# One hybrid mLSTM encoder layer: the seventh block product gets a PSUM bank of its own, and log sigmoid's series runs on 128 partitions behind the first plain pair

## The chip, the cores and the metric

One Trainium2 chip, of which the kernel uses one core. The metric is the device time of one execution in microseconds (us); lower is better. A run of the program gives one time, and the profiler's execution gives a time of its own beside the trace.

## The reference, cut to what matters

A layer of a streaming encoder works on 512 prompt and 32 sample rows (544 in all) of 2048 features, in float32. `h` is the normed and modulated input, and one combined projection `proj = h @ w_in` gives q, k, v, o, z_a, the input and forget gates (2 x 4 columns), u, z_b, g_a and g_b. Two things of it matter here.

```python
ig = ifg[..., :N_HEADS_A].transpose(0, 2, 1)
lf = jax.nn.log_sigmoid(ifg[..., N_HEADS_A:]).transpose(0, 2, 1)   # one value per head and row: 4 x 544
...
b = jnp.cumsum(lf, axis=-1)          # per chunk; b, ig and a running max m set all weights of the mLSTM
proj = jnp.einsum('bld,de->ble', h, w_in)                          # 2048 x 14344 weights
```

Everything behind that (mLSTM, pooling mixer, two branches, output projection, norm) is left as it is by the change.

## The kernel before, in words

The 2048 features lie on 16 tiles of 128 partitions, the 544 rows along the free dimension in two halves of 272. Each float32 operand is split into a rounded high part and a low part (`split`, L91: ScalarE casts the high part, L92, VectorE subtracts to get the low part, L93), and a product of two operands is three matmuls: high by high, high by low, low by high.

**Plain pairs.** The first four pairs of 128 output columns of g_a are computed directly (`plain_pair`, L535, and a first one written out, L477 to L515). A block takes 96 matmuls of 272 columns on TensorE (L547). The first of these pairs also brings the eight gate columns; they are copied to `gsb`, four strips of 4 partitions x 544 (high parts of i and f, then their low parts), at L510 to L513. While the other three pairs run, `sums_of_halves` (L517) prepares on VectorE and ScalarE the sums that the fast pairs need.

**Gates.** Behind the plain pairs in the program (L561 to L635) stand the gates: biases (L565), log sigmoid of f by a series on 4 x 544 elements (L568 to L579), scans (L582, L593), rows of exponents, 21 small transposes on TensorE (L630) and their copies to `tokv` (L633).

**Fast pairs.** The other 50 pairs of blocks of `w_in` go through `fast_pair` (L653), Strassen's scheme in Winograd's form: seven products of half the depth instead of eight. A product (`mul`, L662) is 24 matmuls of 128 x 128 weights and 272 columns, and its weights are the split parts of a block or of a combination of blocks (`parts`, L446, from a pool of three buffers). Three PSUM banks hold the results: `b` and `c` from a pool of two (tiles named mm) and `d` from the auxiliary pool. Products 1 and 4 add up in `b`, 2 and 6 in `d`, and 3, 5 and 7 in `c`. Between 5 and 7 VectorE reads `c` for a sum of its own (`u3`), and only after it may product 7 add to `c`:

```python
            mul(c, parts(t3), S3, False)      # product 5
            plus(u3, c, m1)                   # VectorE reads c
        ...
        mul(c, parts(t4), A22, False)         # product 7 adds to the same bank
        plus(y[0][:, 1, :], c, m1)
```

Here and below the numbers 1 to 7 count the products in the order of the code: b11, t1, t2, b21, b22, t3, t4 are their weights (product 6, b22, runs ahead of product 5, t3, in all pairs but the last). Beside most pairs run `biases` (L774): VectorE sums of rows of `w_in` (`bacc`, L146, L148).

**Order.** Each engine runs its own queue in order. A scheduling layer sets the order within each queue when the program is built, from the order of the code, so that work of one pair can stand among that of the next. DMAs are issued from SP (weights) and POOL (stores of results; in order as well).

Of the kernel before, what the change touches and what calls it, by code (L numbers as in the profile page):

```python
# [9 lines left out]
F32 = mybir.dt.float32  # L10
F32R = mybir.dt.float32r
AF = mybir.ActivationFunctionType
ALU = mybir.AluOpType
# [3 lines left out]
P = 128  # L17
# [4 lines left out]
T = TP + TS  # L22
HALF = T // 2
H = 4
# [27 lines left out]
def body(  # L52
# [9 lines left out]
    act, dve, pool_e, pe, sp = nc.scalar, nc.vector, nc.gpsimd, nc.tensor, nc.sync  # L62
# [6 lines left out]
    dram = ctx.enter_context(tc.tile_pool(name="dram", bufs=1, space=DRAM))  # L69
# [9 lines left out]
    def aux(name):  # L79
        return psum["ax"].tile([P, 512], F32, tag="aux", name=name)  # L80
# [121 lines left out]
    bi = const.tile([H, 1], F32, name="bi")  # L202
    bf = const.tile([H, 1], F32, name="bf")
# [5 lines left out]

    rows_g = dram.tile([H, T], F32, name="rows_g")  # L210
    rows_a = dram.tile([H, TS], F32, name="rows_a")
    d_a = dram.tile([KT, P, T], F32, name="d_a")
    d_tb = dram.tile([KT, P, T], F32, name="d_tb")
    d_ga = dram.tile([KT, P, T], F32, name="d_ga")
# [22 lines left out]
    with ExitStack() as st:  # L237
# [22 lines left out]
        for g in range(2):  # L260
            dve.tensor_tensor(out=cs[:, :, g], in0=vecT[:, 16 * g:16 * g + 16], in1=sg[:, 16 * g:16 * g + 16],
                              op=ALU.mult)
# [183 lines left out]
    def parts(src):  # L446
        whi = wh.tile([P, HK, P], F32R, tag="whi", name="whi")
        wlo = wh.tile([P, HK, P], F32R, tag="wlo", name="wlo")
        split(src, whi, wlo)
        return whi, wlo  # L450
# [66 lines left out]
    def sums_of_halves():  # L517

        for j in range(HK):
            x = []  # L520
            for jj in (j, j + HK):
                t = t2.tile([P, T], F32, tag="hx", name="hx")
                dve.tensor_tensor(out=t, in0=h_hi[:, jj, :].bitcast(F32), in1=h_lo[:, jj, :].bitcast(F32), op=ALU.add)
                x.append(t)
            yield
            (a11, a21), (a12, a22) = ((t[:, 0:HALF], t[:, HALF:T]) for t in x)
            sx = t2.tile([P, 3, HALF], F32, tag="sx", name="sx", bufs=1)
            for dst, p, q, op in ((sx[:, 0, :], a21, a22, ALU.add), (sx[:, 1, :], sx[:, 0, :], a11, ALU.subtract),
                                  (sx[:, 2, :], a12, sx[:, 1, :], ALU.subtract),
                                  (s3[:, j, :], a11, a21, ALU.subtract)):  # L530
                dve.tensor_tensor(out=dst, in0=p, in1=q, op=op)
            split(sx, S_hi[:, :, j, :], S_lo[:, :, j, :])
            yield

    def plain_pair(src, c0, evac, side):  # L535

        raw = [load_rows(src, c0, half) for half in range(2)]
        for blk in range(2):
# [9 lines left out]
                                      start=(k == 0 and x == 0), stop=(k == KT - 1 and x == 2))  # L548
            evac(blk, [acc[:, s, 0:HALF] for s in range(2)])

    side = sums_of_halves()
    for jj in range(1, NPLAIN):
        def evac(blk, acc):
            gate_out(2 * jj + blk, acc)
        plain_pair(w_in_, OFF_GA + jj * 2 * P, evac, side)
    for _ in side:
        pass
    t2_ctx.close()
# [1 line left out]

    g_ctx = ExitStack()  # L561
    g1 = g_ctx.enter_context(tc.tile_pool(name="g1", bufs=1, reuse_waits="tile"))
    ig, fx, t0, t1 = (gsb[:, x, :] for x in range(4))
    for dst, lo, bias in ((ig, t0, bi), (fx, t1, bf)):
        dve.scalar_tensor_tensor(out=dst, in0=dst, scalar=bias, in1=lo, op0=ALU.add, op1=ALU.add)  # L565

    lf = g1.tile([H, T], F32, name="lf")
    dve.scalar_tensor_tensor(out=t0, in0=fx, scalar=-1.0, in1=fx, op0=ALU.mult, op1=ALU.min)  # L568
    act.activation(out=t0, in_=t0, func=AF.Exp)
    dve.tensor_scalar(out=t1, in0=t0, scalar1=2.0, scalar2=None, op0=ALU.add)  # L570
    dve.reciprocal(out=t1, in_=t1)
    dve.tensor_tensor(out=t0, in0=t0, in1=t1, op=ALU.mult)
    dve.tensor_tensor(out=t1, in0=t0, in1=t0, op=ALU.mult)
    dve.tensor_scalar(out=lf, in0=t1, scalar1=2.0 / 19, scalar2=2.0 / 17, op0=ALU.mult, op1=ALU.add)
    for c in (15, 13, 11, 9, 7, 5, 3, 1):
        dve.tensor_tensor(out=lf, in0=lf, in1=t1, op=ALU.mult)
        dve.tensor_scalar(out=lf, in0=lf, scalar1=2.0 / c, scalar2=None, op0=ALU.add)
    dve.tensor_tensor(out=lf, in0=lf, in1=t0, op=ALU.mult)
    dve.scalar_tensor_tensor(out=lf, in0=fx, scalar=0.0, in1=lf, op0=ALU.min, op1=ALU.subtract)  # L579

    mrow = g1.tile([H, T], F32, name="mrow")
    dve.tensor_tensor_scan(out=mrow[:, 0:TP], data0=lf[:, 0:TP], data1=ig[:, 0:TP], initial=0.0,  # L582
                           op0=ALU.add, op1=ALU.max)
# [69 lines left out]
    def fast_pair(src, c0, first, last, side=None, inner=None, final=False):  # L653

        r1, r2 = load_rows(src, c0, 0), load_rows(src, c0, 1)
        b11, b12, b21, b22 = r1[:, :, 0:P], r1[:, :, P:2 * P], r2[:, :, 0:P], r2[:, :, P:2 * P]
        b, c = (psum["mm"].tile([P, 2, 512], F32, tag="mm", name="mm")[:, 0, 0:HALF] for _ in range(2))
        d = aux("d")[:, 0:HALF]  # L660

        def mul(o, w, x, start):  # L662
            for k in range(HK):
                for n, (i, j) in enumerate(((0, 0), (0, 1), (1, 0))):
                    pe.matmul(o, lhsT=w[i][:, k, :], rhs=x[j](k), start=start and k == 0 and n == 0,  # L665
                              stop=k == HK - 1 and n == 2, skip_group_check=not start)

        def quarter(tag):
            return ep.tile([P, HALF], F32, tag=tag, name=tag)

        def plus(o, p, q):
            dve.tensor_tensor(out=o, in0=p, in1=q, op=ALU.add)  # L672

        m1, s5, u2, u3 = (quarter(x) for x in ("m1", "m5", "u2", "u3"))
        y = [y3.tile([P, 2, HALF], F32, tag="y", name="y") for _ in range(2)]
        def step():
            if side is not None:
                next(side, None)

        mul(b, parts(b11), A11, True)  # L680
        act.copy(out=m1, in_=b)
        t1 = combine(b12, b11, ALU.subtract)
        mul(d, parts(t1), S1, True)
        act.copy(out=s5, in_=d)
        t2 = combine(b22, t1, ALU.subtract)
        mul(c, parts(t2), S2, True)
        plus(u2, c, m1)
        step()

        def fourth():  # L690
            mul(b, parts(b21), A12, False)
            first(y[0][:, 0, :], b)

        def fifth():
            t3 = combine(b22, b12, ALU.subtract)
            mul(c, parts(t3), S3, False)
            plus(u3, c, m1)
            step()

        def sixth():  # L700
            mul(d, parts(b22), S4, False)
            plus(y[1][:, 0, :], d, u2)
            step()

        if final:
            fifth()
            fourth()
            sixth()
        else:
            fourth()  # L710
            sixth()
            if inner is not None:
                inner()
            fifth()
        plus(y[1][:, 1, :], u3, s5)
        last(1, y[1])
        t4 = combine(b21, t2, ALU.subtract)
        mul(c, parts(t4), A22, False)
        plus(y[0][:, 1, :], c, m1)
        last(0, y[0])  # L720

    def copy_first(dst, ps):
# [679 lines left out]
```

## Time and profile before

| | us |
|---|---|
| median of 3 runs | 2227.99 (2227.52 to 2229.68) |
| the profiled execution | 2228.75 |
| its span in the trace | 2227.0 |

| engine | busy us | share of the span |
|---|---|---|
| TensorE (PE) | 2182.8 | 98% |
| its weight loads (PEld) | 2115.2 | 95% |
| VectorE (DVE) | 1638.3 | 74% |
| ScalarE (ACT) | 887.1 | 40% |
| GpSimd (POOL) | 121.8 | 5% |

The profile is one execution. Matmuls are pipelined: one lasts 0.29 us in the rows and the next starts 0.125 us behind it, so that a pause of up to 0.16 us between two of them leaves no idle time in the busy share. Starts tell more than busy time here. The plain pairs stand from about 310 to 382 us of the span, the fast pairs from 383 to 1458 us.

### The profile page before, as it was taken

The page shows a single profiled execution, that of the slowest core. Times are in us where ns is not written, and L with a number is a line of the kernel's source. Part 1 is how long each engine was busy: PE and PEld are TensorE (multiplying, and loading weights), DVE is VectorE, ACT ScalarE, POOL GpSimd, SP SyncE. Part 2 cuts the span into 40 slices and gives each one's busy share as a digit, 9 for nine tenths or more (in the row PEclk, how much of TensorE's full clock was granted, in tenths as well). Part 3 has the DMA queues.
Part 4 walks back from the last instruction along what each step waited for, and adds up shares of the span by engine and source line. Part 5 has one row for each costly group of instructions (what it writes and reads, how often), then busy time and mean ns, then how long its engine had stood idle before and what let it go on. Part 6 is the DMA issues. An engine that isn't in the chain of part 4 may idle for free.

```text
span 2227.0 us, 40788 instructions
## 1 busy us (share of the span) xinstructions
PE 2182.8 (98%) x16767; PEld 2115.2 (95%) x16767; DVE 1638.3 (74%) x2422; ACT 887.1 (40%) x1462; POOL 121.8 (5%) x223
## 2 busy tenths in 40 slices
PE   7999999999999999999999999999999989999997
PEld 6899999999999999999999999998788889999997
DVE  5878788987789778977898787666666687774344
ACT  5522344443343343344443444435544442223342
POOL 0000000000000000000000000010011100000000
PEclk9999999999999999999999999999999999999999
DMA  7677643543445334533454333368466477765232
GB/s 242 218 241 237 186 137 112 186 149 122 132 154 168 125 123 139 189 124 125 125 168 150 124 125 116 125 177 272 144 228 231 132 251 227 217 202 185 86 98 97
DMA packets 314170, 366.88 MB, mean 165 GB/s; under 512 B 15296, under 2 KB 257308, under 8 KB 312768
## 3 DMA queue, kind: packets, MB, share of 16 engines
q1 hardware_dynamic: 291368, 306.05, 44.3%
q0 software_dynamic: 20176, 57.63, 7.2%
q8 instruction: 131, 2.15, 0.4%
q10 hardware_dynamic: 2440, 0.61, 0.1%
q14 instruction: 55, 0.45, 0.1%
HBM read 305.53 MB, written 58.67 MB: 164 GB/s over the span
## 4 chain that ended last, share of the span: by engine, by line
PE 88%; DMA 4%; DVE 4%; ACT 2%; issue 1%; SPq 0%; DVEq 0%; ACTq 0%
PE mm L665 31%; PE mm L129 17%; PE d L665 12%; PE mm L131 8%; PE mm L547 3%; PE ca L1031 2%; PE cb L1032 2%; PE mm L907 2%; DMA braw<-in_w_in 2%; PE accp L379 2%; PE mm L1365 2%; PE sc L976 2%; DVE wlo L93 1%; DMA af<-d_a 1%; PE d L501 1%
## 5 line engine op out<-in xcount | busy, mean ns | idle before, releaser
L92 ACT CAST whi<-raw 128x512 fp32r<-128x512 f32 (+1 forms) x426 | 337.0, 796 | 611.2 <-PE mm L129 320.3
L93 DVE TENSOR_TENSOR wlo<-raw,whi 128x512 fp32r<-128x512 f32 (+1 forms) x426 | 383.6, 905 | 226.2 <-ACT whi L92 200.5
L665 PE MATMUL mm<-h_hi,whi 128*128 128x272 f32 x1600 | 465.5, 291 | 1.7 <-DVE u L672 1.7
L665 PE MATMUL mm<-h_lo,whi 128*128 128x272 f32 x1600 | 461.3, 288 | 0.0
L665 PE MATMUL mm<-h_hi,wlo 128*128 128x272 f32 x1600 | 457.5, 290 | 1.5 <-DVE wlo L93 1.3
L92 ACT CAST whi<-t 128x1024 fp32r<-128x1024 f32 x200 | 210.0, 1050 | 392.7 <-PE mm L665 377.1
L665 PEld LDWEIGHTS mm<-h_hi,whi 128*128 128x128 f32 x1600 | 301.3, 188 | 8.1 <-DVE u L672 3.5
L665 PEld LDWEIGHTS mm<-h_lo,whi 128*128 128x128 f32 x1600 | 301.7, 189 | 0.0
L665 PEld LDWEIGHTS mm<-h_hi,wlo 128*128 128x128 f32 x1600 | 298.9, 188 | 2.6 <-DVE wlo L93 2.5
L93 DVE TENSOR_TENSOR wlo<-t,whi 128x1024 fp32r<-128x1024 f32 x200 | 244.8, 1224 | 59.8 <-ACT whi L92 57.9
L665 PE MATMUL d<-S_hi,whi 128*128 128x272 f32 x800 | 230.4, 288 | 1.5 <-ACT whi L92 1.5
L665 PE MATMUL d<-S_hi,wlo 128*128 128x272 f32 x800 | 231.1, 289 | 0.0
L665 PE MATMUL d<-S_lo,whi 128*128 128x272 f32 x800 | 230.6, 288 | 0.0
L665 PEld LDWEIGHTS d<-S_hi,whi 128*128 128x128 f32 x800 | 150.8, 188 | 1.7 <-ACT whi L92 1.7
L665 PEld LDWEIGHTS d<-S_hi,wlo 128*128 128x128 f32 x800 | 151.0, 189 | 0.1
L665 PEld LDWEIGHTS d<-S_lo,whi 128*128 128x128 f32 x800 | 151.0, 189 | 0.0
L650 DVE TENSOR_TENSOR t<-raw,t 128x1024 f32<-128x1024 f32 x100 | 122.2, 1222 | 2.1
L665 PE MATMUL mm<-S_hi,whi 128*128 128x272 f32 x400 | 115.2, 288 | 0.4 <-ACT whi L92 0.4
L665 PE MATMUL mm<-S_hi,wlo 128*128 128x272 f32 x400 | 115.3, 288 | 0.0
L665 PE MATMUL mm<-S_lo,whi 128*128 128x272 f32 x400 | 114.9, 287 | 0.0
L129 PE MATMUL mm<-a_hi,whi 128*128 128x272 f32 x512 | 106.6, 289 | 0.0
L129 PE MATMUL mm<-a_lo,whi 128*128 128x272 f32 x512 | 106.3, 289 | 0.0
(430 smaller groups left out, 4644.8 us busy)
## 6 DMA issues: line engine op xcount, KB each, us to landing
raw<-in_w_in SPq DMA_DIRECT2D x112, 1024.0 KB, 5.4
side<-in_w_ada SPq DMA_DIRECT2D x64, 512.0 KB, 4.7
raw<-in_w_ada SPq DMA_DIRECT2D x32, 512.0 KB, 4.9
braw<-in_w_in SPq DMA_DIRECT2D x64, 256.0 KB, 3.7
raw<-in_w_branch_a SPq DMA_DIRECT2D x32, 512.0 KB, 4.4
raw<-in_w_out SPq DMA_DIRECT2D x32, 512.0 KB, 4.0
d_p<-y POOLq DMA_DIRECT2D x48, 272.0 KB, 3.4
raw<-in_w_in SPq DMA_DIRECT2D x24, 512.0 KB, 5.0
```

Of the source, the lines that this page charges most:

```text
L92: hi_ops.append(act.copy(out=hi, in_=src))
L93: return dve.tensor_tensor(out=lo, in0=src, in1=hi.bitcast(F32), op=ALU.subtract)
L129: pe.matmul(o, lhsT=whi[:, kk, :], rhs=mov[:, k, a:b], start=(k == 0 and mov is hi), stop=False)
L131: pe.matmul(o, lhsT=wlo[:, kk, :], rhs=hi[:, k, a:b], start=False, stop=(k == kt - 1))
L379: pe.matmul(accp[d], lhsT=w[:, d * P:(d + 1) * P], rhs=x[:, j, 0:TP], start=first, stop=last)
L547: pe.matmul(acc[:, s, 0:HALF], lhsT=w[:, kk, :], rhs=mov[:, k, s * HALF:(s + 1) * HALF], start=(k == 0 and x == 0), stop=(k == KT - 1 and ...
L650: dve.tensor_tensor(out=t, in0=p, in1=q, op=op)
L665: pe.matmul(o, lhsT=w[i][:, k, :], rhs=x[j](k), start=start and k == 0 and n == 0, stop=k == HK - 1 and n == 2, skip_group_check=not start)
L907: pe.matmul(acc[:, s, 0:HALF], lhsT=w[:, kk, :], rhs=mov[:, k, s * HALF:(s + 1) * HALF], start=(x == 0 and kk == 0 and y == 0), stop=(x == ...
L976: pe.matmul(sc[:, 0:wd], lhsT=kT[:, d, j * P:(j + 1) * P], rhs=qT[:, d, j * P:TP], start=(d == 0), stop=(d == DB - 1))
L1031: pe.matmul(ca[0:m, 0:HC], lhsT=l, rhs=r[:, 0:HC], start=first, stop=last)
L1032: pe.matmul(cb[0:m, 0:VW - HC], lhsT=l, rhs=r[:, HC:VW], start=first, stop=last)
```

## The change

Product 7 starts a sum of its own in a third PSUM tile, `f`, from the auxiliary pool of four banks, and VectorE adds it to `u3` (which is product 5's bank plus product 1) instead of adding `c` to `m1`. The value is the same sum.

Log sigmoid's series becomes a function that is called behind the second block of the first `plain_pair`. It writes the 4 x 544 strip of f to DRAM (`rows_f`), reads it back as 128 partitions x 17, does the same 24 VectorE operations and the Exp there, writes the result to DRAM (`rows_l`) and reads it back into the strip `t0`, which then stands for `lf`. All four transfers go through POOL's queue. The scans and what follows stay where they were.

```diff
--- before.py
+++ after.py
@@ -209,6 +209,8 @@
 
     rows_g = dram.tile([H, T], F32, name="rows_g")
     rows_a = dram.tile([H, TS], F32, name="rows_a")
+    rows_f = dram.tile([H, T], F32, name="rows_f")
+    rows_l = dram.tile([H, T], F32, name="rows_l")
     d_a = dram.tile([KT, P, T], F32, name="d_a")
     d_tb = dram.tile([KT, P, T], F32, name="d_tb")
     d_ga = dram.tile([KT, P, T], F32, name="d_ga")
@@ -548,11 +550,37 @@
                                       start=(k == 0 and x == 0), stop=(k == KT - 1 and x == 2))
             evac(blk, [acc[:, s, 0:HALF] for s in range(2)])
 
+    ig, fx, t0, t1 = (gsb[:, x, :] for x in range(4))
+
+    def log_sigmoid():
+
+        for dst, lo, bias in ((fx, t1, bf), (ig, t0, bi)):
+            dve.scalar_tensor_tensor(out=dst, in0=dst, scalar=bias, in1=lo, op0=ALU.add, op1=ALU.add)
+        f, e, r, s = (t3.tile([P, H * T // P], F32, name=x) for x in ("lsf", "lse", "lsr", "lss"))
+        pool_e.dma_start(out=rows_f, in_=fx)
+        pool_e.dma_start(out=f, in_=rows_f.rearrange("h t -> (h t)").rearrange("(p c) -> p c", p=P))
+        dve.scalar_tensor_tensor(out=e, in0=f, scalar=-1.0, in1=f, op0=ALU.mult, op1=ALU.min)
+        act.activation(out=e, in_=e, func=AF.Exp)
+        dve.tensor_scalar(out=r, in0=e, scalar1=2.0, scalar2=None, op0=ALU.add)
+        dve.reciprocal(out=r, in_=r)
+        dve.tensor_tensor(out=e, in0=e, in1=r, op=ALU.mult)
+        dve.tensor_tensor(out=r, in0=e, in1=e, op=ALU.mult)
+        dve.tensor_scalar(out=s, in0=r, scalar1=2.0 / 19, scalar2=2.0 / 17, op0=ALU.mult, op1=ALU.add)
+        for c in (15, 13, 11, 9, 7, 5, 3, 1):
+            dve.tensor_tensor(out=s, in0=s, in1=r, op=ALU.mult)
+            dve.tensor_scalar(out=s, in0=s, scalar1=2.0 / c, scalar2=None, op0=ALU.add)
+        dve.tensor_tensor(out=s, in0=s, in1=e, op=ALU.mult)
+        dve.scalar_tensor_tensor(out=s, in0=f, scalar=0.0, in1=s, op0=ALU.min, op1=ALU.subtract)
+        pool_e.dma_start(out=rows_l.rearrange("h t -> (h t)").rearrange("(p c) -> p c", p=P), in_=s)
+        pool_e.dma_start(out=t0, in_=rows_l)
+
     side = sums_of_halves()
     for jj in range(1, NPLAIN):
         def evac(blk, acc):
             gate_out(2 * jj + blk, acc)
         plain_pair(w_in_, OFF_GA + jj * 2 * P, evac, side)
+        if jj == 1:
+            log_sigmoid()
     for _ in side:
         pass
     t2_ctx.close()
@@ -560,24 +588,7 @@
 
     g_ctx = ExitStack()
     g1 = g_ctx.enter_context(tc.tile_pool(name="g1", bufs=1, reuse_waits="tile"))
-    ig, fx, t0, t1 = (gsb[:, x, :] for x in range(4))
-    for dst, lo, bias in ((ig, t0, bi), (fx, t1, bf)):
-        dve.scalar_tensor_tensor(out=dst, in0=dst, scalar=bias, in1=lo, op0=ALU.add, op1=ALU.add)
-
-    lf = g1.tile([H, T], F32, name="lf")
-    dve.scalar_tensor_tensor(out=t0, in0=fx, scalar=-1.0, in1=fx, op0=ALU.mult, op1=ALU.min)
-    act.activation(out=t0, in_=t0, func=AF.Exp)
-    dve.tensor_scalar(out=t1, in0=t0, scalar1=2.0, scalar2=None, op0=ALU.add)
-    dve.reciprocal(out=t1, in_=t1)
-    dve.tensor_tensor(out=t0, in0=t0, in1=t1, op=ALU.mult)
-    dve.tensor_tensor(out=t1, in0=t0, in1=t0, op=ALU.mult)
-    dve.tensor_scalar(out=lf, in0=t1, scalar1=2.0 / 19, scalar2=2.0 / 17, op0=ALU.mult, op1=ALU.add)
-    for c in (15, 13, 11, 9, 7, 5, 3, 1):
-        dve.tensor_tensor(out=lf, in0=lf, in1=t1, op=ALU.mult)
-        dve.tensor_scalar(out=lf, in0=lf, scalar1=2.0 / c, scalar2=None, op0=ALU.add)
-    dve.tensor_tensor(out=lf, in0=lf, in1=t0, op=ALU.mult)
-    dve.scalar_tensor_tensor(out=lf, in0=fx, scalar=0.0, in1=lf, op0=ALU.min, op1=ALU.subtract)
-
+    lf = t0
     mrow = g1.tile([H, T], F32, name="mrow")
     dve.tensor_tensor_scan(out=mrow[:, 0:TP], data0=lf[:, 0:TP], data1=ig[:, 0:TP], initial=0.0,
                            op0=ALU.add, op1=ALU.max)
@@ -715,8 +726,9 @@
         plus(y[1][:, 1, :], u3, s5)
         last(1, y[1])
         t4 = combine(b21, t2, ALU.subtract)
-        mul(c, parts(t4), A22, False)
-        plus(y[0][:, 1, :], c, m1)
+        f = aux("f")[:, 0:HALF]
+        mul(f, parts(t4), A22, True)
+        plus(y[0][:, 1, :], f, u3)
         last(0, y[0])
 
     def copy_first(dst, ps):
```

How this moves instructions, at three places.

TensorE, from the end of product 5 of the second fast pair. Before (mm_4503 is this pair's `c`, mm_4740 the next pair's `b`):

```order
L665 MATMUL mm_4503<-h_lo_104,whi_4668 128x272
L665 MATMUL mm_4503<-h_hi_103,wlo_4669 128x272
L665 MATMUL mm_4740<-h_hi_103,whi_4749 128x272
L665 MATMUL mm_4740<-h_lo_104,whi_4749 128x272
L665 MATMUL mm_4740<-h_hi_103,wlo_4750 128x272
L665 MATMUL mm_4740<-h_hi_103,whi_4749 128x272
L665 MATMUL mm_4740<-h_lo_104,whi_4749 128x272
L665 MATMUL mm_4740<-h_hi_103,wlo_4750 128x272
L665 MATMUL mm_4503<-h_hi_103,whi_4705 128x272
L665 MATMUL mm_4503<-h_lo_104,whi_4705 128x272
```

Now (mm_4513 is `c`, f_4715 the new tile):

```order
L676 MATMUL mm_4513<-h_lo_104,whi_4678 128x272
L676 MATMUL mm_4513<-h_hi_103,wlo_4679 128x272
L676 MATMUL f_4715<-h_hi_103,whi_4716 128x272
L676 MATMUL f_4715<-h_lo_104,whi_4716 128x272
L676 MATMUL f_4715<-h_hi_103,wlo_4717 128x272
```

Before, five or six matmuls of the next pair's product 1 stood between products 5 and 7 (in 46 of the 50 pairs); now product 7 follows product 5, and product 1 of the next pair follows product 7 whole.

VectorE, at the first rows of the series. Before, they stand in the second of the pairs that `plain_pair` computes, between sums of halves (sx, s, hx):

```order
L571 RECIPROCAL gsb<-gsb 4x544
L93 TENSOR_TENSOR wlo<-raw_3627,whi 128x1024
L531 TENSOR_TENSOR sx<-hx 128x272
L572 TENSOR_TENSOR gsb<-gsb 4x544
L531 TENSOR_TENSOR sx<-sx,hx 128x272
L573 TENSOR_TENSOR gsb<-gsb 4x544
```

Now they start a pair earlier (raw_3385 holds weights of the first of them):

```order
L562 SCALAR_TENSOR_TENSOR lse<-lsf 128x17
L525 TENSOR_TENSOR hx<-h_hi,h_lo 128x544
L93 TENSOR_TENSOR wlo<-raw_3385,whi 128x1024
L533 TENSOR_TENSOR sx<-sx,hx 128x272
L533 TENSOR_TENSOR s_2992<-hx 128x272
L564 TENSOR_SCALAR lsr<-lse 128x17
L533 TENSOR_TENSOR sx<-hx,sx 128x272
L565 RECIPROCAL lsr<-lsr 128x17
```

The operation on `lsf` now waits for a DMA, and the split of raw_3385 stands behind it. The scans, which stood behind the end of the series, now stand directly behind the last sum of halves.

POOL, from the load of the gate strips. Before, the six stores of the plain blocks follow each other:

```order
L513 DMA gsb<-gs_3367 4x544 x4
L468 DMA d_ga<-sg 128x544 x6
L586 DMA out<-mrow 4x1
L587 DMA out<-mrow 4x1
L598 DMA rows_g<-gsb 4x544
```

Now:

```order
L515 DMA gsb<-gs_3369 4x544 x4
L470 DMA d_ga<-sg 128x544
L560 DMA rows_f<-gsb 4x544
L470 DMA d_ga<-sg 128x544
L561 DMA lsf<-rows_f 128x17
L470 DMA d_ga<-sg 128x544
L574 DMA rows_l<-lss 128x17
L470 DMA d_ga<-sg 128x544
L575 DMA gsb<-rows_l 4x544
L597 DMA out<-mrow 4x1
```

Each of the four new transfers stands between two stores of plain blocks. On every engine the rest of the order is the same but for a few neighbours that change places.

## Rows read from the trace of the kernel before

**Rows 1.** The profile page: the engines' busy time with its share of the span and the number of instructions.

```profile
PE 2182.8 (98%) x16767; PEld 2115.2 (95%) x16767; DVE 1638.3 (74%) x2422; ACT 887.1 (40%) x1462; POOL 121.8 (5%) x223
```

**Rows 2.** Stretches of the span: its bounds, its length, each engine's busy time with the number of instructions that touch it, the granted share of TensorE's clock, the DMA engines' share, GB/s. The plain pairs; the change to the fast pairs; the first fast pairs, with bias sums beside them; and seven quiet pairs.

```profile
309.80:381.90 72.10, 72.10 (x578) 71.95 (x576) 64.12 (x111) 31.43 (x40) 5.88 (x11) 1.00 0.37 113
381.90:393.00 11.10, 9.21 (x67) 8.62 (x67) 9.29 (x29) 5.19 (x7) 0.54 (x1) 0.85 0.35 103
393.00:470.35 77.35, 77.10 (x611) 76.54 (x610) 73.87 (x91) 33.31 (x43) 3.25 (x6) 1.00 0.57 181
470.35:619.20 148.85, 148.85 (x1177) 147.96 (x1176) 108.56 (x113) 58.37 (x73) 7.57 (x14) 1.00 0.39 126
```

**Rows 3.** One quiet fast pair on the time line, TensorE (start us, length us, engine, line, operation): the last matmul ahead of product 7, its first (0.39) and its second. Then the first matmul of product 7 in the last pair of this kind.

```profile
491.42 0.29 PE L665 MATMUL mm<-h_lo,whi 128*128 128x272 f32 x1
491.61 0.39 PE L665 MATMUL mm<-h_hi,whi 128*128 128x272 f32 x1
491.84 0.29 PE L665 MATMUL mm<-h_lo,whi 128*128 128x272 f32 x1
...
1434.73 0.40 PE L665 MATMUL mm<-h_hi,whi 128*128 128x272 f32 x1
```

**Rows 4.** VectorE on the same time line, with the idle time before an operation and what ended it: the low part of product 7's weights, and `u3`.

```profile
486.06 1.23 DVE L93 TENSOR_TENSOR wlo<-t,whi 128x1024 fp32r<-128x1024 f32 x1 [0.56 <-ACT whi L92]
491.12 0.44 DVE L672 TENSOR_TENSOR u<-mm,m 128x272 f32<-128x272 f32 x1 [0.82 <-PE mm L665]
```

**Rows 5.** Pairs with more to wait for, TensorE: the first of seven in which VectorE's `u3` comes late (what stands ahead of product 7, its first and its second matmul), and product 7's first matmul in the last of them.

```profile
427.51 0.29 PE L665 MATMUL mm<-h_hi,wlo 128*128 128x272 f32 x1
428.04 0.39 PE L665 MATMUL mm<-h_hi,whi 128*128 128x272 f32 x1 [0.25 <-DVE u L672]
428.27 0.29 PE L665 MATMUL mm<-h_lo,whi 128*128 128x272 f32 x1
...
1179.02 0.40 PE L665 MATMUL mm<-h_hi,whi 128*128 128x272 f32 x1 [0.25 <-DVE u L672]
```

**Rows 6.** TensorE and VectorE where the next pair's product 1, moved ahead of product 7, finds the low part of its weights late.

```profile
426.83 0.29 PE L665 MATMUL mm<-h_lo,whi 128*128 128x272 f32 x1
427.03 0.39 PE L665 MATMUL mm<-h_hi,wlo 128*128 128x272 f32 x1
...
1134.59 0.39 PE L665 MATMUL mm<-h_hi,wlo 128*128 128x272 f32 x1 [0.91 <-DVE wlo L93]
1133.32 1.21 DVE L93 TENSOR_TENSOR wlo<-raw,whi 128x1024 fp32r<-128x1024 f32 x1
```

**Rows 7.** The series on VectorE in the plain stretch (line, operation, shapes, count | busy us, mean ns | idle us before), and the smallest operation there.

```profile
L576 DVE TENSOR_TENSOR lf<-lf,gsb 4x544 f32<-4x544 f32 x8 | 5.7, 708 | 0.2
L571 DVE RECIPROCAL gsb<-gsb 4x544 f32<-4x544 f32 x1 | 3.5, 3533 | 0.0
L577 DVE TENSOR_SCALAR lf<-lf 4x544 f32<-4x544 f32 x8 | 3.4, 429 | 0.2
L613 DVE TENSOR_TENSOR dif<-brow,mrow 4x1 f32<-4x1 f32 x1 | 0.1, 143 | 0.0
```

**Rows 8.** The time line there, several engines: a split of weights and the product that first uses it, the end of the gates' rows, and the transposes.

```profile
317.53 1.21 DVE L93 TENSOR_TENSOR wlo<-raw,whi 128x1024 fp32r<-128x1024 f32 x1
328.18 0.41 PE L547 MATMUL mm<-h_hi,wlo 128*128 128x272 f32 x2
374.24 0.66 ACT L620 ACTIVATE gsb<-gsb 4x544 f32<-4x544 f32 x1
381.89 0.78 PE L630 MATMUL tp<-ident,rrow 4*128 4x4 f32 x10
```

**Rows 9.** The change to the fast pairs, VectorE, ScalarE and TensorE.

```profile
383.28 1.52 DVE L633 COPY tokv<-tp 128x4 f32<-128x4 f32 x21 [2.82 <-PE tp L630]
384.73 1.20 DVE L650 TENSOR_TENSOR t<-raw 128x1024 f32<-128x1024 f32 x1
386.54 0.39 ACT L681 COPY m<-mm 128x272 f32<-128x272 f32 x1 [2.52 <-issue]
386.82 2.00 ACT L92 CAST whi<-t 128x1024 fp32r<-128x1024 f32 x2
386.17 0.29 PE L665 MATMUL mm<-h_hi,wlo 128*128 128x272 f32 x1
387.92 0.39 PE L665 MATMUL d<-S_hi,whi 128*128 128x272 f32 x1 [1.46 <-ACT whi L92]
...
392.43 0.43 PE L665 MATMUL d<-S_lo,whi 128*128 128x272 f32 x1
392.65 0.33 PE L665 MATMUL d<-S_hi,wlo 128*128 128x272 f32 x1
```

**Rows 10.** POOL's queue: the nearest round trip through DRAM (a write, and the read that waits for it), its landings, and the stores of plain blocks (KB each, median us to landing).

```profile
370.36 0.53 POOL L621 DMA_DIRECT2D rows_a<-arow  x1
373.53 0.56 POOL L622 DMA_DIRECT2D aB<-rows_a  x1 [2.64 <-DMA rows_a<-arow]
DMA to landing us min/median/max: 2.6/2.9/3.3
d_ga<-sg POOLq DMA_DIRECT2D x8, 272.0 KB, 2.5
d_p<-kT POOLq DMA_DIRECT2D x1, 1088.0 KB, 10.2
```

## The prediction

> **What bounds the kernel now.** I read the busy shares first: TensorE 98%, no other engine over 74% [rows 1]. A gain must therefore come out of TensorE's own time: fewer matmuls, or smaller pauses between them. The change leaves the number of matmuls as it is, so I looked for pauses, and for those the busy share is blind, because a matmul lasts 0.29 us while the next starts 0.125 us behind it. The view of stretches gives the yardstick: the plain pairs do 576 matmuls in 72.10 us, 0.1252 us each, at full granted clock [rows 2]. Seven quiet fast pairs are 7 x 168 = 1176 matmuls, 147.2 us by that yardstick; they take 148.85 [rows 2]. So 0.24 us are lost per pair, at a busy share of 100%.
>
> The time line of one pair shows where. The first matmul of product 7 starts 0.19 us behind the one ahead of it, 0.065 too late, lasts 0.39 instead of 0.29, and the next one comes 0.23 behind it, 0.105 too late [rows 3]. What it waits for is `u3` on VectorE: that runs from 491.12 to 491.56, and the matmul starts at 491.61 [rows 3, 4]. The second part, 0.105, I read as a weight load that could not be started ahead because the instruction was waiting. Together 0.17 of the 0.24 us; the rest is in small steps elsewhere that the change doesn't touch.
>
> **The bank of its own, term by term.** 46 of the 50 pairs have this place; I take the other four at nothing (in two of them other work on TensorE covers the wait, in one eleven matmuls stand between, in the last the products have another order).
> - 33 quiet pairs, from 470.35 to 1434.73 (product 7's start in a middle one and in the last stands in [rows 3]): 33 x 0.17 = 5.6 us.
> - Seven pairs in which VectorE has sums of bias rows in its queue and `u3` comes late, from 428.04 to 1179.02: a step of 0.53, then 0.23, so 0.405 + 0.105 = 0.51 each [rows 5]; 7 x 0.51 = 3.6 us.
> - Six pairs in between (starts at 406, 449, 662, 877, 898 and 920 us, excess of 0 to 0.29 us by the same reading): 0.7 us.
> - The five or six matmuls of the next pair's product 1 that stood ahead of product 7 needed the low part of their weights early. In seven pairs it was late, by 0.07 us in the smallest but one and by 1.07 in the largest, where the matmul at 1134.59 starts when the split begun at 1133.32 is done [rows 6]; 2.9 us in all, with the short step behind each. Now that product comes a whole product, 3.0 us, later, which is more than the largest delay.
>
> Sum 5.6 + 3.6 + 0.7 + 2.9 = 12.8 us. For it to come true product 7 must find nothing else to wait for. Its low weights are ready at 486.06 + 1.23 = 487.29 [rows 4]; without the interleaved matmuls it would start at about 490.95, so 3.6 us are to spare. Its bank comes from a pool of four, in which the product before that used it ended a pair ago. VectorE does as many operations as before on the same sizes. In the pairs with bias sums VectorE is the tight engine, 73.87 of 77.35 us [rows 2]; it still has some 3 us of lead over the products, and the change adds nothing to it.
>
> **The series, term by term.** On 4 partitions it is 24 VectorE operations: a reciprocal of 3.53 us, ten or so two-operand ones of 0.71, about ten of 0.43 [rows 7], some 17 us. On 128 x 17 elements I have no row; the nearest ones are 0.14 us for 4 x 1 elements from below [rows 7] and a 32nd of the old price, or no gain at all, from above, so between 3.4 and 17 us; I take 0.15 us each, 4 us, as 17 elements per partition are nearest to the small row. VectorE thus gets about 13 us free in the plain stretch. That is worth nothing: TensorE does its 576 matmuls there without a pause [rows 2]. Two table loads on ScalarE fall away, at the same worth.
>
> The series also ends earlier, but nobody waits for it: the last row of the gates is ready at 374.24 + 0.66, and the transposes stand behind the plain pairs on TensorE, at 381.89 [rows 8], in the old order and in the new one. So the pause at the change to the fast pairs stays: the copies to `tokv` follow the transposes, the combination for product 2 follows those on VectorE, its cast stands behind the copy of product 1 on ScalarE, and TensorE waits 1.46 us for it; then the granted clock falls to the lower level (0.85 in the stretch) [rows 2, 9]. From 386.17 to 392.65 there are nineteen steps, 2.4 us by the yardstick, in 6.48 us: 4.1 us lost, before and after.
>
> What the four transfers cost: VectorE reaches the operation on `lsf` at about 317 us. A round trip of this kind on POOL took 370.36 to 373.53 to issue the read, with landings of 2.6 to 3.3 us [rows 10], so about 6 us; the strip of f is ready near 311, and the data land at about 317 too. If VectorE waits, the split of weights behind it (317.53 before) waits with it, but TensorE first uses that at 328.18 [rows 8]: 328.18 - 317.53 - 1.21 = 9.4 us of cover. The stores of plain blocks that queue behind these transfers on POOL have buffers that are needed a block, 12 us, later. I take all of this at nothing.
>
> **Forecast.** The profiled execution took 2228.75 us, span 2227.0; minus 12.8 that is 2215.95 and a span of 2214.2. The median of the runs is 0.76 lower than the profiled execution, so the median should be **2215.2 us**.
>
> **Rivals.**
> - *The weight load stays exposed* (chance 0.07). If the first matmul of a product in a fresh bank pays the 0.105 us anyway, 46 x 0.105 = 4.8 us come back: 2220.0. Against it: product 2, which also starts in another bank, starts without such a step in the quiet pairs, or 148.85 us could not hold.
> - *The pause at the change goes too* (0.05). A few tenths of a us earlier there would also spare the clock: up to 4.1 us more, 2211.1. Against it: the order on three engines is the same [rows 9].
> - *Product 7 waits for its weights instead* (0.05), so that nothing is gained: 2228.0. The 3.6 us to spare speak against it.
> - *VectorE is held behind the new round trip*, the one that ends slower (0.02). Place: the operation on `lsf`. Beyond 9.4 us of wait TensorE stands still in the plain pairs. It costs the whole gain when each of the two landings takes about 14 us; at 20 us the wait is 34 us, TensorE stands 25, and a stretch at half clock adds 1.4 (below): 2241 us. The longest landing on this queue was 10.2 us, of 1088 KB [rows 10]. The Trainium skill has a rule that would bring this about ("SBUF — State Buffer", section "Who interferes with whom"): a DMA issued from GpSimd needs descriptors that GpSimd writes, and GpSimd is locked out while VectorE holds the port pair that they share. By that rule a transfer could wait as long as VectorE is busy. In the plain stretch VectorE is busy for 64 of 72 us and the stores from POOL landed 2.5 us after issue at the median [rows 2, 10], so the trace does not bear it out; and a VectorE that waits is idle.
> - *Another bank in the cycle lowers the clock* (0.01). Ahead of 392.65 there are fourteen steps of 0.22 to 0.23 us instead of 0.125 [rows 9]: this fall cost 1.4 us; one in each of 50 pairs would be 70 us, 2285 us in all, and nine of them would eat the gain. The six changes of bank in each pair now go at a granted clock of 1.00 [rows 2]. The Trainium skill ("TensorE: Matmul & The Clock Gate", section "A second HAM failure mode: psum-queue depth-cycling") tells of a kernel whose cycling through banks made TensorE pause often enough for its clock to swing; the trace shows no such swing.
>
> **How the numbers follow.** The forecast gets 0.80. The range reaches from 2210 (the pause at the change gone, and a little more) to 2220 (the weight load still exposed); it leaves out the three cases that end at 2228 or above, 0.08. A measurement of this kernel can tell 0.2%, 4.5 us, from no change. Faster by more than that: forecast and first two rivals, 0.92; within it: the third, 0.05; slower: the last two, 0.03.
>
> **What would show it.** Right: on the time line product 7's first matmul starts 0.125 us behind product 5's last and lasts 0.29; seven quiet pairs take about 147.6 us instead of 148.85; the fast stage is 12 to 13 us shorter, and the stretch up to 382 us and everything behind the fast pairs are as long as before. The wait of ScalarE's cast behind the transposes is still there. Wrong: a step over 0.19 us at product 7's start in the quiet pairs, matmuls of the plain pairs over 0.126 us apart, a granted clock under 1.00 between 470 and 1200 us, or a stage other than the fast one that changes by over 2 us.

## The result: faster by 0.65%, as forecast

The changed kernel takes 2214.55 us (median of 4 runs, 2212.43 to 2218.42) against 2228.84 (2227.52 to 2232.72), a ratio of 0.9935 with a 95% interval of 0.9922 to 0.9948. The forecast was 2215.2 us. The span of its trace is 2214.2 us, and 2214.2 was forecast. That the span agrees to the digit is partly luck, as this table shows. It cuts both spans at the starts of the first and the last matmul of the plain pairs and of the fast stage, and the fast stage itself after 168 matmuls and ahead of its last 168; "again" is a second execution of the same two programs, traced later.

| us | before | before again | changed | changed again |
|---|---|---|---|---|
| up to the plain pairs | 309.64 | 308.83 | 308.15 | 308.58 |
| plain pairs | 72.03 | 72.03 | 72.03 | 72.03 |
| from there to the fast stage (transposes) | 1.49 | 1.49 | 1.49 | 1.49 |
| first fast pair | 25.46 | 25.44 | 25.07 | 23.73 |
| 48 pairs | 1028.59 | 1028.54 | 1015.30 | 1015.30 |
| last fast pair | 21.10 | 21.13 | 21.09 | 21.09 |
| behind the fast stage | 768.66 | 768.55 | 771.04 | 767.67 |
| span | 2226.98 | 2226.02 | 2214.18 | 2209.90 |

The 48 pairs are 13.3 us shorter in the first traces and 13.2 in the second. What lies outside them moves by some us between two executions of one program.

**Profile after.** The stretches that answer to [rows 2], cut at the same places of the program:

```profile
308.15:380.25 72.10, 72.10 (x578) 72.10 (x576) 50.07 (x112) 29.96 (x39) 7.97 (x15) 1.00 0.37 114
380.25:391.50 11.25, 9.40 (x70) 8.77 (x70) 9.33 (x29) 3.91 (x6) 0.54 (x1) 0.85 0.35 104
391.50:468.85 77.35, 77.35 (x619) 77.35 (x618) 74.77 (x92) 34.25 (x44) 3.25 (x6) 1.00 0.58 184
468.85:616.41 147.56, 147.56 (x1178) 147.56 (x1177) 108.52 (x113) 58.39 (x72) 7.56 (x14) 1.00 0.40 127
```

VectorE has lost 14 us of work in the plain pairs (50.07 instead of 64.12), and these last as long as before. Seven quiet pairs take 147.56 us instead of 148.85, at a busy share of 100% in both.

One quiet pair on the time line, to hold against [rows 3, 4]: TensorE around product 7's start, its weight load (PEld), and VectorE's low weights for it and `u3`.

```profile
487.94 0.29 PE L676 MATMUL mm<-h_hi,wlo 128*128 128x272 f32 x1
488.06 0.29 PE L676 MATMUL f<-h_hi,whi 128*128 128x272 f32 x1
488.19 0.29 PE L676 MATMUL f<-h_lo,whi 128*128 128x272 f32 x1
487.94 0.19 PEld L676 LDWEIGHTS f<-h_hi,whi 128*128 128x128 f32 x1
483.21 1.23 DVE L93 TENSOR_TENSOR wlo<-t,whi 128x1024 fp32r<-128x1024 f32 x1 [0.56 <-ACT whi L92]
488.26 0.44 DVE L683 TENSOR_TENSOR u<-mm,m 128x272 f32<-128x272 f32 x1 [0.82 <-PE mm L676]
```

Product 7's first matmul starts 0.12 us behind product 5's last and lasts 0.29, while VectorE reads product 5's bank for `u3` only afterwards, at 488.26. Its weights are loaded 0.12 us ahead of it, and the low part was ready at 484.44, 3.6 us early. The waits that leave TensorE idle, from the plain pairs to the end of the fast stage (who waits, for whom: us in total, times, longest), first those before:

```profile
PE mm L665 <- DVE u L672: 1.7, 7, 0.2
PE d L665 <- ACT whi L92: 1.5, 1, 1.5
PE mm L665 <- DVE wlo L93: 1.3, 2, 0.9
PE mm L665 <- ACT whi L92: 0.4, 1, 0.4
```

Now two are left, and both stand at the change to the fast pairs:

```profile
PE d L676 <- ACT whi L92: 1.4, 1, 1.4
PE mm L676 <- ACT whi L92: 0.4, 1, 0.4
```

The series on VectorE (count, busy us, mean ns, idle us before and whose), and the round trip on POOL's queue ahead of it:

```profile
L570 DVE TENSOR_TENSOR lss<-lss,lsr 128x17 f32<-128x17 f32 x8 | 1.4, 172 | 0.0
L571 DVE TENSOR_SCALAR lss<-lss 128x17 f32<-128x17 f32 x8 | 1.4, 169 | 0.0
L565 DVE RECIPROCAL lsr<-lsr 128x17 f32<-128x17 f32 x1 | 0.3, 255 | 0.0
L562 DVE SCALAR_TENSOR_TENSOR lse<-lsf 128x17 f32<-128x17 f32 x1 | 0.2, 180 | 1.9 <-DMA lsf<-rows_f 1.9
...
309.62 0.50 POOL L560 DMA_DIRECT2D rows_f<-gsb  x1 [3.56 <-DVE gsb L558]
311.92 0.56 POOL L561 DMA_DIRECT2D lsf<-rows_f  x1 [1.22 <-DMA rows_f<-gsb]
```

An operation on 128 x 17 elements takes 0.17 us (0.15 taken, 0.43 to 0.71 on 4 x 544 in [rows 7]). VectorE waits 1.9 us for the data, which come at 316.6 us, and TensorE does not notice.

The change to the fast pairs, to hold against [rows 9]:

```profile
381.79 1.53 DVE L644 COPY tokv<-tp 128x4 f32<-128x4 f32 x21 [2.82 <-PE tp L641]
385.00 0.39 ACT L692 COPY m<-mm 128x272 f32<-128x272 f32 x1 [3.76 <-PE mm L676]
385.28 2.00 ACT L92 CAST whi<-t 128x1024 fp32r<-128x1024 f32 x2
386.39 0.39 PE L676 MATMUL d<-S_hi,whi 128*128 128x272 f32 x1 [1.42 <-ACT whi L92]
386.62 0.29 PE L676 MATMUL d<-S_lo,whi 128*128 128x272 f32 x1
```

The chain is the same, and so is the wait, 1.42 us instead of 1.46.

### The profile page after: what moved, and what is told of

It reads as the page before. It is cut to its first block, busy times and chain, and to the rows that moved or that the text cites. A ratio compares the mean times of both kernels' runs of the same rounds, so it can differ in the third digit from the quotient of the medians.

```text
span 2214.2 us, 40739 instructions
## 1 busy us (share of the span) xinstructions
PE 2174.1 (98%) x16767; PEld 2114.2 (95%) x16767; DVE 1621.5 (73%) x2422; ACT 885.1 (40%) x1460; POOL 123.9 (6%) x227
## 4 chain that ended last, share of the span: by engine, by line
PE 93%; DMA 2%; DVE 2%; ACT 1%; issue 0%; SPq 0%; DVEq 0%; ACTq 0%
PE mm L676 27%; PE mm L129 16%; PE d L676 14%; PE mm L131 8%; PE f L676 7%; PE mm L549 3%; PE ca L1043 2%; PE cb L1044 2%; PE mm L919 2%; PE accp L381 2%; PE sc L988 2%; PE mm L1377 2%; PE ada L295 1%; PE d L503 1%; DMA af<-d_a 0%
## 5 line engine op out<-in xcount | busy, mean ns | idle before, releaser
L676 PE MATMUL mm<-h_hi,wlo 128*128 128x272 f32 x1200 | 347.5, 290 | 0.0
L676 PE MATMUL mm<-h_lo,whi 128*128 128x272 f32 x1200 | 345.7, 288 | 0.0
L676 PE MATMUL mm<-h_hi,whi 128*128 128x272 f32 x1200 | 345.5, 288 | 0.0
L676 PEld LDWEIGHTS mm<-h_lo,whi 128*128 128x128 f32 x1200 | 226.1, 188 | 0.0
L676 PEld LDWEIGHTS mm<-h_hi,whi 128*128 128x128 f32 x1200 | 225.7, 188 | 0.1
L676 PEld LDWEIGHTS mm<-h_hi,wlo 128*128 128x128 f32 x1200 | 225.6, 188 | 0.0
L676 PE MATMUL f<-h_lo,whi 128*128 128x272 f32 x400 | 115.6, 289 | 0.0
L676 PE MATMUL f<-h_hi,wlo 128*128 128x272 f32 x400 | 115.0, 288 | 0.0
L676 PE MATMUL f<-h_hi,whi 128*128 128x272 f32 x400 | 114.9, 287 | 0.0
```

## The experiments

The table gives the stages of each trace as above (plain pairs with the step to the fast stage; "rest" is the 48 pairs). Times are medians, with the ratio to the kernel before and its interval.

| | plain | first pair | rest | last | behind | median, ratio |
|---|---|---|---|---|---|---|
| bank alone | 73.52 | 23.80 | 1015.30 | 21.10 | 768.25 | 2214.25, 0.9934 (0.9914 to 0.9955) |
| series alone | 73.52 | 25.38 | 1028.09 | 21.10 | 772.71 | 2230.67, 1.0010 (0.9994 to 1.0025) |
| sum in d | 73.52 | 25.26 | 1015.31 | 21.90 | 770.60 | 2217.36, 0.9947 (0.9932 to 0.9962) |
| sum in c | 73.52 | 23.87 | 1028.06 | 21.10 | 772.33 | 2230.11, 0.9999 (0.9990 to 1.0008) |
| transposes early | 73.63 | 21.09 | 1015.31 | 21.11 | 771.58 | 2212.79, 0.9926 (0.9914 to 0.9939) |
| the same, old series | 75.71 | 21.11 | 1015.30 | 21.09 | 769.15 | 2215.39, 0.9943 (0.9929 to 0.9958) |
| four round trips | 73.52 | 23.76 | 1015.30 | 21.11 | 768.54 | 2211.97 (one run) |
| products 5 and 4 exchanged | 73.52 | 25.26 | 1022.62 | 21.11 | 769.94 | 2221.80, 0.9966 (0.9954 to 0.9979) |

**The two halves of the change.** The bank alone is the kernel before with these lines (the code is cut to what differs, here and below):

```diff
-        mul(c, parts(t4), A22, False)
-        plus(y[0][:, 1, :], c, m1)
+        f = aux("f")[:, 0:HALF]
+        mul(f, parts(t4), A22, True)
+        plus(y[0][:, 1, :], f, u3)
```

> The kernel before with product 7 in a tile of its own, and the series as it was. Theory (the whole gain comes from product 7 no longer waiting for u3): the fast stage, from its first to its last matmul, takes 1061.5 us as in the changed kernel (1075.1 before), seven quiet pairs 147.6, and the median is about 2215 us, ratio 0.994. Rival (the series moved to 128 partitions brings part of it): the fast stage stays over 1064 us, or another stage is over 2 us longer than in the changed kernel.

The series alone is the changed kernel with the same lines turned back.

> The changed kernel with product 7 back in bank c, behind u3; only the series is moved. Theory (VectorE's free time in the plain stretch is worth nothing): the plain pairs take 72.0 us as before, the fast stage 1075 us, the median is 2228 us within 2, ratio 1.000. VectorE waits some 2 us for the data of the first round trip, and TensorE does not notice. Rival (the series is worth something): a fast stage or a plain stretch shorter by over 1 us, median under 2225.

The bank alone gives the whole gain: its 48 pairs take 1015.30 us like the changed kernel's. The series alone gives none. Its 48 pairs differ by 0.5 us from those of before, in pairs beside which bias sums run and which go up and down by 0.2 to 0.4 us each.

**Own sum or own bank.** Product 7 starts a sum anew in both, in a bank that has been read (d) or in one that has not (c):

```diff
-        mul(f, parts(t4), A22, True)
-        plus(y[0][:, 1, :], f, u3)
+        mul(d, parts(t4), A22, True)        # sum in c: c instead of d
+        plus(y[0][:, 1, :], d, u3)
```

> The changed kernel, but product 7 starts its own sum in bank d, which product 6 has left and VectorE has read a product earlier, so that no third tile is needed. Theory (what counts is that the bank needn't be waited for, not that it is a further one): fast stage 1061.5 us, median 2214.5, ratio 0.9935. Rival (a third tile matters, since d is still being read or the bank is switched more often): a step of over 0.15 us at the start of product 7 in quiet pairs, 0.1 to 0.17 each, fast stage 1066 to 1070 us, median 2219 to 2223.

> The changed kernel, but product 7 starts its sum anew in bank c, which VectorE has to read first for u3. The sum is its own, the bank is not. Theory (the wait for u3 costs, and with it the weight load behind the wait): as before the change, a step of 0.19 us and then one of 0.23 at product 7's start in the quiet pairs, fast stage 1075 us, median 2228, ratio 1.000. Rival (adding to a sum that was read in between is what costs): fast stage 1062 us, median 2215.

Bank c brings the old steps back, TensorE's matmuls and weight loads in a quiet pair:

```profile
487.90 0.29 PE L676 MATMUL mm<-h_lo,whi 128*128 128x272 f32 x1
488.10 0.40 PE L676 MATMUL mm<-h_hi,whi 128*128 128x272 f32 x1
488.33 0.29 PE L676 MATMUL mm<-h_lo,whi 128*128 128x272 f32 x1
487.78 0.19 PEld L676 LDWEIGHTS mm<-h_lo,whi 128*128 128x128 f32 x1
488.10 0.19 PEld L676 LDWEIGHTS mm<-h_hi,whi 128*128 128x128 f32 x1
```

Here the load starts together with the matmul that had to wait (488.10), not 0.12 us ahead as for the one before it (487.78 and 487.90), and that matmul lasts 0.11 us longer. So it is not adding to an old sum that costs, since a new sum in bank c costs as much; waiting for the read does.

Why does the load wait for that read, when its weights have long been ready (in the kernel before at 487.29 us [rows 4], for a load at 491.61)? In the traces the wait stands on the load itself: of the 16767 matmuls of the kernel before none carries a wait of its own. Where the wait is long enough to show in the rows of the weight loads (the late `u3` of [rows 5]), they name VectorE's `u` as what ended it:

```profile
427.38 0.19 PEld L665 LDWEIGHTS mm<-h_hi,wlo 128*128 128x128 f32 x1
428.04 0.19 PEld L665 LDWEIGHTS mm<-h_hi,whi 128*128 128x128 f32 x1 [0.47 <-DVE u L672]
```

So the load did not go ahead because the program, as it is built, makes the load wait too. No run here has a wait on the matmul alone, so whether the load would then go ahead, and save its 0.1 us without another bank, stays open.

Bank d needs no further tile and gives the same 48 pairs. Only in the last pair, where just five matmuls of the next stage (L918) stand between product 6 and product 7, product 7 waits for VectorE's read of d (1440.53 to 1440.97):

```profile
1440.83 0.29 PE L918 MATMUL mm<-h_hi,wlo 128*128 128x272 f32 x1
1441.03 0.40 PE L676 MATMUL d<-h_hi,whi 128*128 128x272 f32 x1
1441.26 0.29 PE L676 MATMUL d<-h_lo,whi 128*128 128x272 f32 x1
```

That is 0.18 us of the 0.8 by which this last pair is longer; the rest is the five matmuls themselves, work of the next stage. The median of this version is 3 us above that of the bank alone; in the traces of the two the difference lies outside the 48 pairs.

**The same wait at another place.**

```diff
-        if final:
+        if True:
             fifth()
             fourth()
             sixth()
```

This version leaves out the difference of halves (S3), so that its output is not that of the layer.

> The changed kernel with products 5 and 4 exchanged in every fast pair, as they stand in the last pair already. Product 5 then adds to bank c while VectorE reads it for u2, the kind of wait that product 7 had before, at another place; some matmuls of product 4 stand in between. The last pair of the changed kernel shows it with steps of 0.193 and 0.228 us, 0.17 lost. Theory (a matmul that waits for VectorE's read costs its wait and then the weight load that was not started ahead, wherever it stands): the same two steps in each quiet pair, seven quiet pairs 147.56 + 7 x 0.17 = 148.8 us, the fast stage 49 x 0.17 = 8.4 us longer than in the changed kernel, 1068.5 to 1070 us, more if the bias sums make u2 late, and the median about 2221 us. Rival (the loss of before belonged to product 7's place at the end of a pair, among the next pair's matmuls): seven quiet pairs 147.6 us, fast stage under 1063, median 2213.

Its quiet pairs take 21.23 us instead of 21.08, but its first pair takes 32.66: without that difference, bias sums run on VectorE already in the plain stretch, and the copies stand behind them. Its median, 2229.64 us, is that of the kernel before (ratio 1.0003, 0.9990 to 1.0015). VectorE there, and TensorE's wait:

```profile
385.57 1.41 DVE L148 SCALAR_TENSOR_TENSOR bacc<-braw,mod,bacc 128x512 f32<-128x512 f32 x2 [0.37 <-DMA braw<-in_w_in]
386.90 1.52 DVE L644 COPY tokv<-tp 128x4 f32<-128x4 f32 x21
...
PE d L676 <- ACT whi L92: 6.9, 1, 6.9
```

So it was run again with the difference in it (`if inner is not None: inner()` ahead of `fifth()`); the table has this run.

> Products 5 and 4 exchanged once more, now with the difference of halves (S3) computed ahead of product 5 in the first pair, which the run before left out; without it bias sums stood ahead of the copies to tokv in VectorE's queue, and the first pair took 32.7 us. Theory (0.152 us for each of 48 pairs, as in that run, and nothing else): first pair 23.7 to 25.1 us, quiet pairs 21.23, fast stage 1067.4 to 1069 us, median 2218 to 2222, ratio 0.997. Rival (the exchange costs elsewhere too): first pair over 25.5 us, or the stretch behind the fast pairs longer than the 767.2 to 772.7 us of the other traces.

```profile
480.56 0.29 PE L676 MATMUL mm<-h_lo,whi 128*128 128x272 f32 x1
480.75 0.39 PE L676 MATMUL mm<-h_hi,whi 128*128 128x272 f32 x1
480.98 0.29 PE L676 MATMUL mm<-h_lo,whi 128*128 128x272 f32 x1
```

The signature of [rows 3] now stands at product 5's start, in the middle of the pair, and the 48 pairs are 7.3 us longer than in the changed kernel, 0.152 each. The wait has its price at this place too, a little under that at product 7 (0.183, below).

**A longer round trip.** Three more writes and reads of `rows_f`:

```diff
+        for _ in range(3):
+            pool_e.dma_start(out=rows_f..., in_=f)
+            pool_e.dma_start(out=f, in_=rows_f...)
```

> The changed kernel with the strip of f sent through DRAM and back three times more ahead of the series, so that the data come some 20 us later. The order of VectorE's queue puts the series about 18 us later for it. Theory (the round trip has cover, and the series' end has slack up to the transposes at 380 us): VectorE waits under 5 us, plain pairs 72.0 us, fast stage 1060 to 1062 us, nothing changes. Rival (VectorE is held behind the round trip): a wait of VectorE of over 9 us, the plain pairs 3 to 13 us longer, and a granted clock under 1.00 there.

VectorE's waits there:

```profile
DVE mrow L596 <- DMA gsb<-rows_l: 4.9, 1, 4.9
DVE lse L565 <- DMA lsf<-rows_f: 4.0, 1, 4.0
```

No stage is longer. The scheduling layer put the series further back in VectorE's queue (its first operation runs at 333.31 us, 316.62 in the changed kernel), so that this run says nothing of what a wait beyond the cover would cost; it says that a late landing alone does not make one.

**The transposes early.** The code of the gates, from the scans to the copies to `tokv`, becomes a function:

```diff
         def evac(blk, acc):
             gate_out(2 * jj + blk, acc)
+            if jj == NPLAIN - 1 and blk == 0:
+                for _ in side:
+                    pass
+                t2_ctx.close()
+                gates()
```

> The changed kernel with the code of the gates (scans, rows, 21 transposes, copies to tokv) called behind the first block of the last plain pair instead of behind the last block. The rows are ready at 355 us since the series is early, so TensorE finds them ready; the copies, the combination for product 2 and its cast then come before the last plain block ends. Theory (the pause of 1.7 us and the wait of 0.6 behind it stand there only because the transposes stand behind the plain pairs): the first fast pair takes 21.1 to 21.3 us instead of 23.8 to 25.1, the granted clock stays 1.00 there, the whole is 2.6 to 3.9 us shorter than the changed kernel, about 2211 us. Rival (something else is late there too, the cast behind the last sigmoids or the split of S3): the pause only shrinks, first pair over 22 us, median within 1.5 us of the changed kernel's 2214.5.

> The same place for the transposes, with the bank of its own, but log sigmoid's series on 4 partitions as in the kernel before. Its rows are ready only at about 372 us, some 5 us into the last plain block. Theory (13 us less of VectorE's time are worth something once the transposes stand early): TensorE waits 1 to 3 us for the rows among the matmuls of the last block, which lasts 13 to 15 us instead of 12, and half of the gain at the change to the fast pairs is lost: 2212 to 2215 us. Rival (the series is worth nothing here either): as with the series on 128 partitions, plain pairs 73 us long with the transposes in them, first fast pair 21.2 us, about 2211 us.

TensorE does the transposes between two blocks without a wait, and the cast for product 2 is ready at 376.33, 8 us before it is used; the first pair and its clock:

```profile
367.89 0.78 PE L630 MATMUL tp<-ident,rrow 4*128 4x4 f32 x10
368.53 0.71 PE L630 MATMUL tp<-ident,gsb 4*128 4x4 f32 x11
375.28 1.05 ACT L92 CAST whi<-t 128x1024 fp32r<-128x1024 f32 x1 [5.90 <-PE mm L549]
384.33 0.28 PE L680 MATMUL d<-S_hi,whi 128*128 128x272 f32 x1
...
381.30:402.40 21.10, 21.10 (x171) 21.10 (x170) 18.89 (x25) 8.85 (x13) 0.54 (x1) 1.00 0.49 147
```

The first pair loses nothing any more: plain pairs and first pair take 94.72 us instead of 97.25 or 98.59, the two values of the changed kernel. With the old series the rows come later, and the last block waits:

```profile
367.36 0.22 PE L621 MATMUL tp<-ident,rrow 4*128 4x4 f32 x1 [0.48 <-DVE rrow L597]
367.78 1.25 PE L621 MATMUL tp<-ident,rrow 4*128 4x4 f32 x8 [0.19 <-DVE rrow L599]
```

That costs 2.1 us (75.71 against 73.63): 0.7 of it is the two waits shown, the rest lies in transposes that come singly over the block, with steps of 0.18 to 0.32 us. So the series' move is worth 2.1 us, but only once the transposes stand early.

Is this version faster than the changed kernel? Both were run once more, side by side.

> The changed kernel as it is, beside the version with the early transposes, to compare the two on one chip. All theories: plain pairs 72.0 us, the first fast pair between 23.7 us (granted clock 1.00 behind the pause) and 25.1 (clock lowered), the other 49 fast pairs 1036.4 us as in the first trace; median 2214.5 within 2.

> The version with the early transposes once more. Theory: plain pairs and fast stage together 1131.1 us, 2.6 to 3.9 us shorter than in the changed kernel, and the median of the same session lower by that, about 0.15%. Rival (what is gained there is given back behind the fast pairs or is below what the runs can tell): medians within 1 us of each other.

> The kernel before as it is, for a second trace of it: which stages differ between two executions of the same program. Theory: the 48 fast pairs between the first and the last take 1028.1 to 1028.6 us as in the traces with product 7 in bank c; what differs by over 1 us is the start (up to 50 us), the first fast pair and the stretch behind the fast pairs, 1500 to 1580 us, where the granted clock is not 1.00. Rival: the fast pairs themselves differ by several us between executions.

The traces repeat: 94.73 us against 97.25. The times cannot tell it: 2211.86 us (2207.51 to 2216.14) against 2211.78 (2209.92 to 2213.11), ratios to before 0.9925 (0.9911 to 0.9940) and 0.9927 (0.9913 to 0.9940). The 2.5 us lie below what the parts outside the stage vary by.

## Why the prediction was right, point by point

- **Quiet pairs**: 33 x 0.17 = 5.6 us was the term. Measured are the same 33 pairs with 0.183 each, 6.0 us; the small steps that I had put elsewhere were partly its own.
- **The pairs with late `u3`, the six in between, and the late low parts of product 1**: 3.6 + 0.7 + 2.9 = 7.2 us was the sum. The other 15 of the 48 pairs gave 7.3 us, and the first pair, which has one of the six places, 0.4. These were forecast from one execution; against "series alone" and "sum in c", whose bias sums ran a little otherwise, the 15 pairs would have given 6.7.
- **The exposed weight load** (0.105 us of each 0.17) was a reading, and PEld's rows show it. The Trainium skill ("TensorE: Matmul & The Clock Gate", section "Step-by-step: what each phase is for") says that weight loads are pulled ahead of running matmuls; the trace agrees, 0.12 us ahead. What it adds is that the load at product 7's start, which carries the wait, did not go ahead. The rival that a fresh bank pays it anyway is out: 488.06 to 488.19 is a normal step.
- **Product 7 waits for its weights instead**: out, 3.6 us to spare as worked out.
- **The series is worth nothing in the plain stretch**: right, 72.03 us in every trace with the transposes at their place. VectorE got 14 us free (13 forecast).
- **The pause at the change stays**: right in kind, 1.42 us of wait. Of the 4.1 us lost there, 1.3 hang on the clock, which did not fall in every execution: see below. The rival that the pause goes needed another place of the transposes; the early transposes show that the time lost there can be won.
- **VectorE held behind the round trip**: the data came at 316.6 us (about 317 forecast; two small errors cancel here, since the strip left at 309.62, not near 311, and the trip took 7 us, not 6), and the wait of 1.9 us stayed under the 9.4 of cover. The rival's working left out that the scheduling layer moves the waiting operation when the data come late, as the longer round trip showed.
- **Another bank lowers the clock**: out, granted clock 1.00 from 391.50 us on in the fast stage.
- **The sum** was 12.8 us for the fast stage, which became 13.7 shorter: 13.3 in the 48 pairs and 0.4 in the first. That is outside the 12 to 13 us that were to show it right, and that the whole span fell by exactly 12.8 is luck: two parts that the change does not touch made up the difference, the start, 1.5 us shorter, and the end, 2.4 longer. The 2.4 us are even one of the prediction's own signs of being wrong (another stage that changes by over 2 us); the sign was drawn too tight, since this stretch takes 767.2 to 773.7 us over all the traces. The second traces repeat neither: there the start is 0.3 us shorter and the end 0.9 shorter. At the end it was a late landing that ScalarE waited for (3.33 us, 1.84 in the second execution, 1.95 before) and a lowered clock behind it (0.91 from 1503 to 1521 us, 1.00 in the second). These rows are of the changed kernel, first and second execution:

```profile
1511.69 0.93 ACT L1155 ACTIVATE qk<-qk,bias 128x512 f32<-128x512 f32 x2 [3.33 <-DMA qk<-d_p]
```

```profile
1509.42 0.93 ACT L1155 ACTIVATE qk<-qk,bias 128x512 f32<-128x512 f32 x2 [1.84 <-DMA qk<-d_p]
```

## What to carry to other kernels

Where TensorE is busy all the time, look at the steps between starts: here a matmul that wrote to a bank which another engine had to read first paid what was left of its wait and a weight load of 0.1 us, and the five or six matmuls put ahead of it hid, in the quiet pairs, most of the wait but not the load. A further bank and one that had already been read did equally well. Time freed on an engine that nobody waits for is worth nothing until what stands behind it in program order is moved too, and a gain of 0.1% (the early transposes) is read from the stage, not from the runs.

## What was not expected of the hardware

Behind the same pause at the change (a step of 1.7 us, then one of 0.7) the clock fell in some executions and not in others. The stretch with the granted clock (its seventh figure) in two executions of the changed kernel:

```profile
380.00:392.00 12.00, 10.15 (x76) 9.52 (x75) 9.83 (x29) 3.98 (x7) 0.54 (x1) 0.86 0.40 116
```

```profile
380.00:392.00 12.00, 10.15 (x87) 9.42 (x86) 9.39 (x29) 4.90 (x8) 0.54 (x1) 1.00 0.35 104
```

At the lower level (1.2 GHz) the steps are 0.227 us, at the upper (2.4) 0.125. Of ten traces with this pause six show the fall (first pair 25.07 to 25.46 us) and four do not (23.73 to 23.87). In the changed kernel it costs 1.3 us (25.07 against 23.73). The three traces with early transposes have no pause there and keep 1.00. What decides it in an execution stays open.
